# One hybrid decoder layer on one core: a new opening with diagonal transposes, larger pipelined side steps, and the second half of the cache staged through scratch

## The chip, the core and the metric

The kernel runs on one core of one Trainium2 chip, as one launch. The time is device microseconds of one execution, and the number compared is the median of several executions. Engines are named as in the profile: PE (TensorE matmul), PEld (its weight loads), DVE (VectorE), ACT (ScalarE), POOL (GpSimd), SP (SyncE, which here issues nearly all DMAs).

## The reference, cut to what matters

One layer of a hybrid decoder runs on 512 prompt tokens and on 32 sample tokens (8 sequences of 4), 544 columns in all. Every branch hangs on one input projection of the normalised tokens:

```
h = rmsnorm(x, norm_w)                    # 544 x 2048
zin = h @ w_in                            # 2048 x 14376, columns split into q, kv, gates, pool, conv, merge
# branch A: attention over compressed blocks, selected blocks and a window; the prompt reads its own keys,
#           a sample sequence reads 2048 past rows from 16 cache pages:
#           cache_kv[page] = 128 rows x (k_cmp, v_cmp, k_slc, v_slc) x 2 heads x 128
# branch B: causal pooling; branch C: conv and a chunked state-space scan
y = x + sum_b(sigmoid(G_b) * (m_b @ w_branch[b])) @ w_out
```

## The kernel before, in words

**Main units.** The projection is cut into tiles of 128 output columns, and each tile into four units of 4 x 128 contraction rows (a tile of the branch projection has two). A unit is one object with three calls: `dma()` loads 512 KB of weights (every second unit), `prep()` splits the weights into a high part `wh` (ACT) and a low part `wl` (DVE), and `mm()` issues 24 matmuls of 272 columns into the accumulator `zin` (wh x hhi, wl x hhi, wh x hlo, for two halves of the 544 columns). `hhi` and `hlo` are the normalised, transposed tokens in two parts. There are 612 units, and `run_units` walks through them: it loads six units ahead, prepares three units ahead, and then issues unit i.

**Side steps.** Everything else (norms of q and k, attention, pooling, convolution, scan, sample attention) is written as generators that stop at `yield`. After each unit, `run_units` adds `s.rate` to a counter and for each whole one takes one step of every generator in `s.sides`. The Tile scheduler then makes one instruction order for each engine out of this, and may pull instructions past each other where it thinks that one isn't ready. On PE the side matmuls therefore stand as insertions in a long row of `zin` matmuls. All side accumulators share four PSUM buffers (`s.A`, tag "a"), and most side data shares 32 SBUF buffers (`s.U`).

**Opening.** `x_prep` loads the sample tokens and four blocks of 128 prompt tokens, squares them (ACT), computes the reciprocal root (DVE, with one ACT Sqrt), scales the block by it and by `norm_w` (DVE, `scalar_tensor_tensor`), transposes it (PE, L156) into a tile `xT`, and splits it into `hhi` and `hlo`. The first unit needs all four blocks, since a matmul of 272 columns reaches across blocks. The first side generator, `tables`, loads constants and casts them on DVE (`trib`, `identb` and so on).

**Cache pages.** A page's number stands in a table, so a page load takes its address from a register that SP reads first (`value_load`). `stage_pages`, a side generator, copies columns 0 to 511 (the compressed keys and values) of 128 pages into scratch in HBM, `ckd`. The compressed kinds 0 and 1 are then loaded from `ckd` with fixed addresses, and the selected kinds 2 and 3 straight from the pages:

```
u = s.U("kr")
if kind < 2:                       # 256 KB from scratch, fixed address
    nc.sync.dma_start(u[:, :512]..., src[:, 4 * lq + e:4 * lq + e + 2, 256 * kind:256 * kind + 256])
if kind > 1:                       # 128 KB from the page whose number a register holds
    nc.sync.dma_start(u[:, o:o + 256], s.page(t, 4 * bl + e)[:, 256 * kind:256 * kind + 256])
```

SP issues DMAs strictly in its order: a weight load `wr` stands behind the `kr` loads issued ahead of it. The sample attention runs after the prompt attention `attn_p`: `samp_cmp` (keys `kT`, scores `cS`, values `pv`, `xvT`, `ocT`) twice, then `samp_group` four times (window and selected keys `kT`, scores `sS`, transposed probabilities `sP`, sums `sO`).

Of the kernel before, what the change touches and what calls it, by code (L numbers as in the profile page):

```python
# [29 lines left out]
RATE_SSD = 1.7  # L30
RATE_MG = 1.5
# [92 lines left out]
class Prog:  # L124
    def __init__(s, ctx, tc, a):
        s.ctx, s.tc, s.nc = ctx, tc, tc.nc
        s.a = a
        s.n = 0
        s.sides = []
# [67 lines left out]
    def setup(s):  # L197
# [8 lines left out]
        s.rate = 1.0  # L206
# [7 lines left out]
        s.ckd = [dt(f"ckd{b}", [16, 128, 512]) for b in range(8)]  # L214
# [15 lines left out]
    def params(s):  # L230
# [15 lines left out]
        s.nw = s.prm[:, 0:16]  # L246
# [10 lines left out]
        nc.vector.tensor_copy(s.trib, trineg)  # L257
        s.snegb = s.cp0.tile([32, 32], BF, name="snegb")
        nc.vector.tensor_copy(s.snegb, sneg[:32])
        s.identb = s.cp0.tile([128, 128], BF, name="identb")  # L260
        nc.vector.tensor_copy(s.identb, s.c("ident"))
        s.identr = s.cp0.tile([128, 128], R, name="identr")
        nc.vector.tensor_copy(s.identr, s.c("ident"))
# [3 lines left out]
    def x_prep(s):  # L267
        nc, a = s.nc, s.a
        X, J, W = {}, {}, []
        nw = a["norm_w"]  # L270
        row = lambda q, n: bass.AP(tensor=nw.tensor, offset=nw.offset + 512 * q, ap=[[0, n], [1, 512]])
        xs = s.U("xs")
# [3 lines left out]
        nc.sync.dma_start(s.cst[:, :128], a["cst_a"][:, :128])  # L276
        for i in range(4):
            X[i] = [s.U("x") for _ in range(4)]
            for q in range(4):
                nc.sync.dma_start(X[i][q][:, :512], a["x_prompt"][0, i * 128:i * 128 + 128, q * 512:q * 512 + 512])  # L280
            if i == 0:
                w4 = s.U("nw4")
                for q in range(4):
                    nc.sync.dma_start(w4[32 * q:32 * q + 32, :512], row(q, 32))
                mod, = s.cu("mod32")
                for q in range(4):
                    W.append(s.U("nw"))
                    nc.sync.dma_start(W[q][:, :512], row(q, 128))
        yield
# [3 lines left out]
        def square(x, o):  # L293
            j = s.U("junk")
            s.act(j[:, :512], x[:, :512], AF.Square, accum_out=o)


        ss = s.small(8)
        square(xs, ss[:, 0:1])
        p = s.A("xss")  # L300
        s.mm(p[:, :1], mod, ss[:, 0:1])
        nc.vector.tensor_copy(ss[:, 1:2], p[:, :1])
        s.rsqrt(ss[:, 2:3], ss[:, 1:2], 1.0 / DM, ss[:, 3:4])
        s.stt(xs[:, :512], xs[:, :512], ss[:, 2:3], w4[:, :512])
        p = s.A("xT")
        pv = p.rearrange("p (q e c) -> p e q c", q=4, e=4)
        for e in range(4):
            s.tr(pv[:, e], xs[:, e * 128:e * 128 + 128])
        s.hsplit(p.rearrange("p (k c) -> p k c", k=16), s.hhi[:, :, NP:T], s.hlo[:, :, NP:T])

        def norms(i):
            ss = J[i] = s.small(8)
            for q in range(4):
                square(X[i][q], ss[:, q:q + 1])

        def scale(i):
            ss = J.pop(i)
            nc.vector.tensor_reduce(ss[:, 4:5], ss[:, :4], axis=AX.X, op=OP.add)
            s.rsqrt(ss[:, 5:6], ss[:, 4:5], 1.0 / DM, ss[:, 6:7])
            for q in range(4):  # L320
                s.stt(X[i][q][:, :512], X[i][q][:, :512], ss[:, 5:6], W[q][:, :512])

        def turn(i):
            xs = X.pop(i)
            c = slice(i * 128, i * 128 + 128)
            for q in range(4):
                p = s.A("xT")
                for e in range(4):
                    s.tr(p[:, e * 128:e * 128 + 128], xs[q][:, e * 128:e * 128 + 128])
# [3 lines left out]
        for i in range(5):  # L333
            if i < 4:
                norms(i)
            if i:
                turn(i - 1)
# [1584 lines left out]
```

## Time and profile before

| | us |
|---|---|
| median of 3 runs (2452.2 to 2456.29) | 2454.61 |
| the profiled execution's own time | 2455.51 |
| its span, first to last instruction | 2453.7 |
| PE busy | 2381.8 (97%) |
| DVE busy | 1084.9 (44%) |
| ACT busy | 716.9 (29%) |
| POOL busy | 55.7 (2%) |

The profiled execution took 0.9 us more than the median, and 1.8 us of its time lie outside the span. PE is busy nearly all the time. Whatever shortens the kernel therefore takes away PE's idle time, makes its row of matmuls shorter, or lets it run at its faster clock for longer. In the tables of windows, PEclk is the granted clock as a share of 2.4 GHz: 0.50 is 1.2 GHz.

### The profile page before, as it was taken

To read this page: it belongs to the slowest core of one execution; us is meant where nothing else is said; L and a number is where in the kernel's file an instruction comes from. 1 tells how busy PE (TensorE), PEld (TensorE's weight loads), DVE (VectorE), ACT (ScalarE), POOL (GpSimd) and SP (SyncE) were. 2 spreads that over 40 slices of the span, in tenths; PEclk is the share of its full clock that TensorE was granted. 3 is DMA by queue.
4 is the path that set the end of the run, shared out by engine and by line. 5 is a ranking of instruction groups with operands and counts; after the bars stand their busy time and mean duration, and the time that the engine had idled before them with its cause. 6 is when DMAs were issued, how large, how long until landed. Compare 5 with 4: busy or idle time off the path is not lost. (4 is left out here: it accounts for less than half of the span.)

```text
span 2453.7 us, 49120 instructions
## 1 busy us (share of the span) xinstructions
PE 2381.8 (97%) x19749; PEld 2239.6 (91%) x19749; DVE 1084.9 (44%) x2206; ACT 716.9 (29%) x1369; POOL 55.7 (2%) x153
## 2 busy tenths in 40 slices
PE   4999999999999999999899999999999999999999
PEld 4999888888998998988798999989999999999999
DVE  5227547555332232423353545555446344445222
ACT  4222333333332222322232233322223322223221
POOL 0001011000000000000000000000000000000000
PEclk9999899999999999999999999999999999999999
DMA  7855563422568567665656543333646664443442
GB/s 213 243 160 147 168 173 99 136 69 75 154 202 246 159 192 227 174 196 162 208 160 196 143 126 89 102 105 111 183 128 196 183 189 132 133 133 99 127 132 81
DMA packets 525668, 377.27 MB, mean 154 GB/s; under 512 B 26895, under 2 KB 472615, under 8 KB 525440
## 3 DMA queue, kind: packets, MB, share of 16 engines
q1 hardware_dynamic: 518528, 360.76, 51.5%
q10 hardware_dynamic: 6912, 13.37, 1.5%
q8 instruction: 155, 2.54, 0.4%
q14 instruction: 73, 0.60, 0.1%
HBM read 328.31 MB, written 79.66 MB: 166 GB/s over the span
## 5 line engine op out<-in xcount | busy, mean ns | idle before, releaser
L153 PE MATMUL zin<-hhi,wh 128*128 128x272 f32 (+1 forms) x3616 | 784.6, 297 | 5.6 <-ACT wh L173 4.6
L176 DVE TENSOR_TENSOR wl<-wr,wh 128x512 fp32r<-128x512 f32 (+1 forms) x612 | 422.9, 693 | 776.4 <-ACT wh L173 772.9
L153 PE MATMUL zin<-hlo,wh 128*128 128x272 f32 (+1 forms) x3616 | 757.7, 290 | 0.0
L153 PE MATMUL zin<-hhi,wl 128*128 128x272 f32 (+1 forms) x3616 | 756.5, 290 | 0.2 <-DVE wl L176 0.2
L173 ACT ACTIVATE wh<-wr 128x512 fp32r<-128x512 f32 (+1 forms) x612 | 382.9, 628 | 1108.7 <-PE zin L153 919.5
L153 PEld LDWEIGHTS zin<-hhi,wh 128*128 128x128 f32 (+1 forms) x3616 | 568.3, 189 | 38.6 <-issue 28.3
L153 PEld LDWEIGHTS zin<-hhi,wl 128*128 128x128 f32 (+1 forms) x3616 | 570.2, 189 | 4.5 <-issue 3.0
L153 PEld LDWEIGHTS zin<-hlo,wh 128*128 128x128 f32 (+1 forms) x3616 | 567.8, 189 | 6.1 <-issue 5.2
L153 PE MATMUL zin<-bh,wh 128*128 128x272 f32 x1280 | 266.4, 290 | 1.1 <-DVE gt L185 1.1
L153 PE MATMUL zin<-bl,wh 128*128 128x272 f32 x1280 | 264.7, 288 | 0.0
L153 PE MATMUL zin<-bh,wl 128*128 128x272 f32 x1280 | 264.4, 288 | 0.0
L153 PEld LDWEIGHTS zin<-bh,wh 128*128 128x128 f32 x1280 | 200.0, 188 | 1.4 <-ACT wh L173 1.3
L153 PEld LDWEIGHTS zin<-bl,wh 128*128 128x128 f32 x1280 | 201.3, 189 | 0.0
L153 PEld LDWEIGHTS zin<-bh,wl 128*128 128x128 f32 x1280 | 201.1, 188 | 0.0
L1364 DVE COPY kT<-kT 128x512 f32<-128x512 f32 x72 | 49.0, 688 | 63.7 <-PE kT L156 63.1
L156 PE MATMUL kT<-cst,kr 128*128 128x128 f32 x512 | 68.9, 276 | 0.0
L156 PEld LDWEIGHTS kT<-cst,kr 128*128 128x128 f32 x512 | 56.6, 141 | 7.7 <-issue 5.7
L173 ACT ACTIVATE mg<-zin 128x544 f32<-128x544 f32 x48 | 29.8, 620 | 101.9 <-PE zin L153 101.9
L173 ACT ACTIVATE P<-S,sm 128x512 f32<-128x512 f32 (+3 forms) x64 | 33.8, 528 | 86.6 <-DVE sm L182 84.3
L173 ACT ACTIVATE kT<-kT 128x512 f32<-128x512 f32 x72 | 42.5, 595 | 33.8 <-PE kT L156 33.2
L153 PE MATMUL S<-kv,q 128*128 128x128 f32 (+3 forms) x128 | 47.1, 452 | 0.2
L153 PE MATMUL O<-PT,Vn 128*128 128x128 f32 x320 | 44.4, 277 | 0.0
(409 smaller groups left out, 1839.4 us busy)
## 6 DMA issues: line engine op xcount, KB each, us to landing
wr<-in_w_in_dram SPq DMA_DIRECT2D x224, 512.0 KB
ckd<-in_cache_kv_dram SPq DMA_DIRECT2D x128, 256.0 KB
kr<-ckd SPq DMA_DIRECT2D x128, 256.0 KB
kr<-in_cache_kv_dram SPq DMA_DIRECT2D x256, 128.0 KB
wr<-in_w_branch_dram SPq DMA_DIRECT2D x48, 512.0 KB
wr<-in_w_out_dram SPq DMA_DIRECT2D x32, 512.0 KB
mgd<-mg ACTq DMA_DIRECT2D x48, 272.0 KB
gt<-mgd SPq DMA_DIRECT2D x48, 272.0 KB
```

Source lines behind the costliest of these rows:

```text
L153: return s.nc.tensor.matmul(out, l, r, start=start, stop=stop, **kw)
L156: return s.nc.tensor.transpose(out, in_, s.c("ident")[:k, :k])
L173: return s.nc.scalar.activation(out, in_, f, **kw)
L176: return (eng or s.nc.vector).tensor_tensor(out, a, b, op=op)
L1364: s.nc.vector.tensor_copy(u[:, :NP], p)
```

## The change

Three things are done at once.

1. The opening is written anew and in an order fixed by hand (`manual_schedule` for ACT, DVE, PE and SP). Blocks 0 and 1 are loaded first. A block is no longer scaled on DVE. Its reciprocal root is multiplied into an identity matrix (`dg`), and an ordinary matmul of the block with that diagonal transposes and scales it in one; `norm_w` comes in when the result is split. The first tile's accumulator is split into 256 columns (blocks 0 and 1) and 288 columns (blocks 2, 3 and the samples), so that units 0 to 3 issue their first half (`part(q, 0)`) before blocks 2 and 3 are turned, and the second half (`part(q, 1)`) between their banks. Four casts of `tables` move from DVE to POOL.
2. Side steps are made larger: several old steps are one, and a step uses what the step before it produced. The rate falls from 1.0 (1.5 and 1.7 in places) to 0.55 (0.75 late). Page staging and the early loads of the branch stage move to a list of their own, `s.feeds`, which takes one step after each unit.
3. `stage_pages` copies both halves of the 128 pages into scratch (256 copies in place of 128), and the selected kinds are loaded from there, 128 loads of 256 KB in place of 256 of 128 KB.

```diff
-RATE_SSD = 1.7
-RATE_MG = 1.5
+RATE = 0.55
+RATE_SSD = 0.75
...
-        nc.vector.tensor_copy(s.trib, trineg)
+        nc.gpsimd.tensor_copy(s.trib, trineg)
...
+        load(0)
+        load(1)
+        units[0].dma()
+        units[2].dma()
...
+        def root(ss, n, i0):
+            v, r, t = ss[:, 16:16 + n], ss[:, 19:19 + n], ss[:, :n]
+            s.act(r, v, AF.Sqrt)
+            nc.vector.reciprocal(r, r)
...
+                s.ts(D[i0 + i][:, :128], ident, r[:, i:i + 1])
+        def split(*kpc):
+            for k, p, c in kpc:
+                s.act(s.hhi[:, k, c], p, scale=nwT[:, k:k + 1])
+            for k, p, c in kpc:
+                s.stt(s.hlo[:, k, c], p, nwT[:, k:k + 1], s.hhi[:, k, c].bitcast(F), OP.mult, OP.subtract)
...
+        def bankA(kb):
+            p = s.A("xT")
+            for h in range(2):
+                k = 2 * kb + h
+                for i in range(2):
+                    s.mm(p[:, h * 256 + i * 128:h * 256 + i * 128 + 128],
+                         X[i][k // 4][:, k % 4 * 128:k % 4 * 128 + 128], D[i][:, :128])
+            return p
...
+        bank = [bankA(kb) for kb in range(4)]
+        for kb in range(8):
+            split(*((2 * kb + h, bank[kb][:, h * 256:h * 256 + 256], slice(0, 256)) for h in range(2)))
+            if kb < 4:
+                bank.append(bankA(kb + 4))
+            if kb % 2:
+                units[kb // 2].prep()
+                part(kb // 2, 0)
+            if kb == 3:
+                square(xs, sc[:, 12:13])
+                p = s.A("xss")
+                s.mm(p[:, :1], mod, sc[:, 12:13])
+            if kb == 4:
+                nc.vector.memset(sc[:, 8:12], 0.0)
+                nc.vector.tensor_copy(sc[:, 8:9], p[:, :1])
+            if kb > 3:
+                i, q = divmod(2 * kb - 8, 4)
+                square(X[2 + i][q], sc[:, 4 * i + q:4 * i + q + 1])
+                square(X[2 + i][q + 1], sc[:, 4 * i + q + 1:4 * i + q + 2], True)
...
+        mean(sc, 3)
+        root(sc, 3, 2)
+        bank = [bankB(k) for k in range(4)]
+        for k in range(16):
+            split((k, bank[k][:, :288], slice(256, T)))
+            if k < 12:
+                bank.append(bankB(k + 4))
+            if k % 4 == 3:
+                part(k // 4, 1)
...
-                s.nc.sync.dma_start(s.ckd[b][i], s.page(t, i)[:, :512])
-                yield
+        for k in range(2):
+            for b in range(8):
+                t, nx = nx, s.ids((b + 1) % 8, 1, 0, 16)
+                for i in range(16):
+                    s.nc.sync.dma_start(s.ckd[k][b][i], s.page(t, i)[:, 512 * k:512 * k + 512])
+                    yield
...
                 units[i].mm()
+                s.feeds = [g for g in s.feeds if next(g, s) is not s]
                 acc += s.rate
...
+        for n in range(0, 36, 2):
+            for f, d in ((sc, 4), (sb, 2), (sa, 0)):
+                for m in (n - d, n - d + 1):
+                    if 0 <= m < 32:
+                        f(m)
             yield
...
+        for n in range(9):
+            if n:
+                scores(n - 1, kT)
+                kT = None
+            if n < 8:
+                kT = s.keys4(need(), CI)
+            yield
...
-            if j + 2 < 8:
-                W[j + 2] = s.cmp_w(1, j + 2)
+            if j + 3 < 8:
+                W[j + 3] = s.cmp_w(1, j + 3)
...
-            yield from keyT(need(), got)
+            p = scores(kT)
             u = s.U("sS")
...
+            if lq < 3:
+                kT = s.keys4(need(), CI)
+                yield
```

What the change does to the order, at three places. First DVE in the opening, before the change: the row in which the last block's root (the small `sm_298` rows) is mixed with weight splits `wl` and with the casts `trib` and `snegb` of the side generator.

```order
59 L176 TENSOR_TENSOR wl_354<-wr_151,wh_353 128x512
60 L191 RECIPROCAL sm_298<-sm_298 128x1
61 L176 TENSOR_TENSOR wl_358<-wr_153,wh_357 128x512
62 L176 TENSOR_TENSOR sm_298<-sm_298 128x1
63 L176 TENSOR_TENSOR wl_392<-wr_153,wh_391 128x512
64 L176 TENSOR_TENSOR sm_298<-sm_298 128x1
65 L257 CAST trib<-cu_430 128x128
66 L182 TENSOR_SCALAR sm_298<-sm_298 128x1
67 L259 CAST snegb<-cu_430 32x32
68 L176 TENSOR_TENSOR sm_298<-sm_298 128x1
```

The same engine in the opening after the change, between the fourth and the sixth bank of the first half (`hlo` rows are the low part of a turned bank, `junk` rows are squares, `xss` is PE's sum for the samples):

```order
23 L176 TENSOR_TENSOR wl_278<-wr_127,wh_277 128x512
24 L185 SCALAR_TENSOR_TENSOR hlo<-xT_229,sm_163,hhi 128x256 x2
25 L393 MEMSET sm_168 128x4
26 L394 COPY sm_168<-xss_295 128x1
27 L312 SCALAR_TENSOR_TENSOR junk_305,sm_168<-x_139 128x512
28 L185 SCALAR_TENSOR_TENSOR hlo<-xT_238,sm_163,hhi 128x256 x2
29 L176 TENSOR_TENSOR wl_312<-wr_129,wh_311 128x512
30 L312 SCALAR_TENSOR_TENSOR junk_329,sm_168<-x_141 128x512
```

The casts are gone from DVE, and the copy of `xss` now stands ahead of the rest of the first half's work.

Second, PE in the first group of the sample attention before the change: scores `sS` alone between two rows of main matmuls.

```order
4030 L153 MATMUL zin_12327<-hlo,wh_12230 128x272 x2
4031 L153 MATMUL sS_12409<-kT_12358,qs 32x512
4032 L153 MATMUL sS_12409<-kT_12365,qs 32x512
4033 L153 MATMUL sS_12409<-kT_12372,qs 32x512
4034 L153 MATMUL sS_12409<-kT_12379,qs 32x512
4035 L153 MATMUL zin_12327<-hhi,wh_12282 128x272 x2
```

PE at the like place after the change: behind the scores (their last row is the first here) stand, in one insertion, the transposes of the new keys and probabilities and those of the next 16 key tiles, in seven accumulators of the four buffers.

```order
4810 L153 MATMUL sS_15328<-kT_15252,qs 32x512
4811 L156 MATMUL nT_15336<-cst,nk_15095 16x128
4812 L156 MATMUL sP_15340<-cst,sW_15214 128x128 x4
4813 L156 MATMUL kT_15355<-cst,kr_14284 128x128 x2
4814 L156 MATMUL kT_15355<-cst,kr_14286 128x128 x2
4815 L156 MATMUL kT_15362<-cst,kr_14284 128x128 x2
4816 L156 MATMUL kT_15362<-cst,kr_14286 128x128 x2
4817 L156 MATMUL kT_15369<-cst,kr_14288 128x128 x2
4818 L156 MATMUL kT_15369<-cst,kr_14290 128x128 x2
4819 L156 MATMUL kT_15376<-cst,kr_14288 128x128 x2
4820 L156 MATMUL kT_15376<-cst,kr_14290 128x128 x2
4821 L153 MATMUL zin_15179<-hhi,wh_15175 128x272 x2
```

Counted over the whole order, PE goes over from main matmuls to an insertion 424 times before and 284 times after the change; from unit 4 on 420 and 278 times. The number of side matmuls from unit 4 on is the same but for two.

Third, SP where the selected rows of the first group are loaded, before the change: each load is preceded by the read of a page number.

```order
888 L350 TENSOR_LOAD pt_11640
889 L350 ISA x2
890 L375 ISA
891 L375 DMA kr_11707<-in_cache_kv_dram 128x256
892 L350 TENSOR_LOAD pt_11640
893 L350 ISA x2
894 L375 ISA
895 L375 DMA kr_11728<-in_cache_kv_dram 128x256
```

After the change such loads come from scratch, four for what were eight, next to the weights and small stores.

```order
1602 L447 DMA kr_17478<-ckd_91 128x2x256
1603 L447 DMA kr_17480<-ckd_91 128x2x256
1604 L447 DMA kr_17482<-ckd_92 128x2x256
1605 L447 DMA kr_17484<-ckd_92 128x2x256
1606 L489 DMA wr_17894<-in_w_in_dram 128x8x128
```

The reads of page numbers have moved to the staging, one page after each unit from unit 4 to unit 260. Measured in units, the prompt attention stands at units 86 to 136 before and 86 to 164 after, the two `samp_cmp` at 139 to 209 and 168 to 258, the four `samp_group` at 211 to 315 and 263 to 333. From unit 455 on (branch and output projection) the two orders do the same.

## Rows read from the trace of the kernel before

**Rows 1.** The page, part 1: engines, busy us, share, instructions.
```profile
PE 2381.8 (97%) x19749; PEld 2239.6 (91%) x19749; DVE 1084.9 (44%) x2206; ACT 716.9 (29%) x1369; POOL 55.7 (2%) x153
```

**Rows 2.** Waits of PE, whole run: us in total, times, longest.
```profile
PE xT L156 <- DVE x L185: 18.3, 5, 9.4
...
PE sS L153 <- ACT kT L173: 5.8, 2, 5.1
PE zin L153 <- ACT wh L173: 4.6, 1, 4.6
PE ocT L153 <- DMA cw<-in_cmp_w_dram: 4.2, 2, 3.4
PE pm L153 <- ACT pwh L173: 3.8, 1, 3.8
PE spT L156 <- ACT pu L173: 3.7, 1, 3.7
...
PE sO L153 <- ACT nT L173: 2.5, 1, 2.5
PE sS L153 <- DVE kT L1364: 2.0, 1, 2.0
```

**Rows 3.** Timeline of PE in the opening; at 60.11 unit 4 begins.
```profile
43.77 3.65 PE L156 MATMUL xT<-cst,x 128*128 128x128 f32 x16 [9.43 <-DVE x L185]
...
60.11 0.41 PE L153 MATMUL zin<-hhi,wh 128*128 128x272 f32 x2
```

**Rows 4.** Timeline of DVE in the opening.
```profile
11.04 0.16 DVE L302 COPY sm<-xss 128x1 f32<-128x1 f32 x1 [6.11 <-PE xss L153]
...
12.43 0.16 DVE L176 TENSOR_TENSOR sm<-sm 128x1 f32<-128x1 f32 x1
...
42.35 0.23 DVE L257 CAST trib<-cu 128x128 bf16<-128x128 f32 x1 [3.66 <-DMA cu<-in_cst_u_dram]
...
45.52 0.69 DVE L176 TENSOR_TENSOR hlo<-xT,hhi 128x512 fp32r<-128x512 f32 x1
```

**Rows 5.** Windows of the opening: engines' busy us, then PEclk, DMA share, GB/s.
```profile
0.00:10.00 10.00, 0.00 (x0) 0.00 (x0) 0.42 (x3) 2.93 (x6) 0.98 (x6) 1.00 0.65 190
...
40.00:48.00 8.00, 4.24 (x20) 4.26 (x21) 5.21 (x11) 2.35 (x4) 0.00 (x0) 0.50 0.55 154
```

**Rows 6.** Timeline of PE around one insertion, and around one of plain fp32 matmuls.
```profile
676.87 0.42 PE L153 MATMUL zin<-hlo,wh 128*128 128x272 f32 x2
677.12 1.04 PE L156 MATMUL kT<-cst,kr 128*128 128x128 f32 x8
677.91 0.49 PE L153 MATMUL zin<-hhi,wh 128*128 128x272 f32 x2
678.25 0.41 PE L153 MATMUL zin<-hhi,wl 128*128 128x272 f32 x2
...
794.84 1.95 PE L153 MATMUL ocT<-xvT,cw 128*128 128x128 f32 x16
```

**Rows 7.** The chain that ended last: a stretch without insertions.
```profile
1969.98 292.13 PE zin L153 x2328
```

**Rows 8.** Windows, columns as in rows 5.
```profile
300.00:600.00 300.00, 297.78 (x2446) 260.73 (x2445) 178.63 (x469) 104.43 (x244) 15.22 (x24) 1.00 0.40 114
755.00:790.00 35.00, 35.00 (x329) 30.35 (x322) 9.98 (x15) 10.10 (x17) 0.00 (x0) 1.00 1.06 311
1100.00:1200.00 100.00, 86.13 (x755) 78.20 (x754) 32.17 (x66) 24.81 (x55) 1.69 (x6) 0.97 0.59 172
1300.00:1400.00 100.00, 95.44 (x818) 88.66 (x819) 44.73 (x94) 27.89 (x56) 9.19 (x28) 0.98 0.60 173
```

**Rows 9.** Timeline of SP: page loads during the sample groups.
```profile
1108.61 8.67 SPq L375 DMA_DIRECT2D kr<-in_cache_kv_dram  x8
```

**Rows 10.** The tile kr, 600 to 1000 us: issue from scratch, ns min/median/max.
```profile
L371 SPq DMA_DIRECT2D kr<-ckd x128: 354/420/1457, 636.1 to 932.8; - x128
```

**Rows 11.** Timeline of ACT behind such page loads.
```profile
1194.63 1.15 ACT L173 ACTIVATE wh<-wr 128x512 fp32r<-128x512 f32 x2 [3.18 <-DMA wr<-in_w_in_dram]
```

More of the change, by code (lines that the diff above doesn't have):

```diff
@@ L275, in x_prep @@
             nc.sync.dma_start(xs[32 * q:32 * q + 32, :512], src[:, q * 512:q * 512 + 512])
[L276 to L288, printed above, removed]
-        yield
+        mod, = s.cu("mod32")
+        load(2)
+        load(3)
+        units[4].dma()
+        units[6].dma()
         dummy = s.small(1)
@@ L307, in x_prep @@
[L307 to L321, printed above, removed]
@@ new lines, in _opening, with part @@
+        ps = s.Z("zin")
+        def part(q, hf):
+            o, n = ((0, 256), (256, 288))[hf]
+            wh, wl = units[q].w
+            for k in range(4):
+                kk = 4 * q + k
+                xh, xl = s.hmov(kk)
+                for m, (w_, x_) in enumerate(((wh, xh), (wl, xh), (wh, xl))):
+                    s.mm(ps[:, hf, :n], w_[:, k], x_[:, o:o + n], kk == 0 and m == 0, kk == 15 and m == 2)
+        def bankA(kb):
[6 more added lines that the diff above has]
+            return p
@@ new lines, in bankB @@
+        def bankB(k):
+            p = s.A("xT")
+            q, e = divmod(k, 4)
+            for i in (2, 3):
+                s.mm(p[:, i * 128 - 256:i * 128 - 128], X[i][q][:, e * 128:e * 128 + 128], D[i][:, :128])
+            r = slice(32 * q, 32 * q + 32)
+            s.mm(p[:, 256:288], xs[r, e * 128:e * 128 + 128], D[4][r, r])
+            return p
+        sa, sb, sc = s.small(24), s.small(24), s.small(24)
+        for q in range(4):
+            square(X[0][q], sa[:, q:q + 1])
+        mean(sa, 1)
@@ new lines, in _opening @@
+        square(X[1][0], sb[:, 0:1])
+        root(sa, 1, 0)
+        for q in range(1, 4):
+            square(X[1][q], sb[:, q:q + 1], q == 2)
+        mean(sb, 1)
+        root(sb, 1, 1)
+        bank = [bankA(kb) for kb in range(4)]
[17 more added lines that the diff above has]
+                square(X[2 + i][q + 1], sc[:, 4 * i + q + 1:4 * i + q + 2], True)
@@ L1272, in m_norm @@
         for g in range(2):
-            P = [s.A("ms") for _ in range(2)]
+            Z = []
             for e in range(4):
@@ new lines, in sums @@
+        def sums(po, pt, raw, o, last):
+            for e in range(4):
+                for ci, bl, g in CI:
+                    v, c = raw[bl, e]
+                    c += o + g * 128
+                    s.mm(po[32 * ci:32 * ci + 32, :128], pt[:, e * 128 + 32 * ci:e * 128 + 32 * ci + 32],
+                         v[:, c:c + 128], False, last and e == 3, skip_group_check=True)
+        kT = s.keys4(wn, CI)
+        yield
+        p = s.A("vn")
+        for br in range(2):
+            s.tr(p[:16, br * 128:br * 128 + 128], vx[:, br])
@@ L1693, in open_e @@
     def open_e(s):
-        while s.sides:
+        while s.sides or s.feeds:
+            s.feeds = [g for g in s.feeds if next(g, s) is not s]
             s.step()
```

590 lines of the change are left out of this document (304 added, 286 removed).

## The prediction

> **What bounds the kernel now.** I first read the shares of busy time: PE is busy 97% of the span, no other engine half of it [rows 1]. So I read PE alone, in three views. The chain that ended last holds a stretch without insertions, 2328 main matmuls in 292.13 us, or 125.5 ns each [rows 7]. At that pace 14688 main matmuls are 1843 us, and the rest is insertions, waits and slow clock. The waits of PE come next [rows 2]: 18.3 us for scaled blocks in the opening, and later a handful of single stalls of 2 to 5 us. The windows show where the clock is lost: 0.50 late in the opening [rows 5], 0.97 and 0.98 in the two stretches with the long stalls [rows 8].
>
> **Term 1, the opening.** Unit 4 begins at 60.11 us [rows 3]; after the change units 0 to 3 are done inside the new opening, so its length is compared with that. What goes is plain: DVE stood 3.66 us for a constant behind which the last block's root and scaling waited [rows 4], and PE then idled 9.43 us and ran 16 transposes in 3.65 us, 0.228 each, twice the 0.13 or less of the eight in 1.04 us later on [rows 3, 6], with the granted clock at 0.50 [rows 5]. What comes, step by step:
>
> - Blocks 0 and 1 are about 2.2 MB with the constants. The queue moved 1.9 MB in its first 10 us [rows 5], so they have landed at about 10.5. Then the last square (about 0.7, as a 512-column row [rows 4]), a sum, the root (11.04 to 12.59, 1.55 us, for the like chain [rows 4]) and the diagonal: PE starts at 13.2.
> - A diagonal transpose is a plain fp32 matmul. Eight of 128 columns, in 16 records, took 1.95 us [rows 6], so 0.22 each with the tail taken off. A bank of the first half is four, 0.88 us. The first four banks I count at half speed, as the 16 transposes went [rows 3]: 7 us, to 20.
> - From there DVE sets the pace. It starts at 15.2, when the first bank is out and its high part copied. Its work in the first half is 16 rows of 256 columns at 0.42 (by the 0.69 of 512 columns [rows 4]), four `wl` and four squares at 0.69 and some small rows, together 12.8 us. Its order also puts the copy of `xss` ahead of half of that, and PE makes `xss` only behind the second part: DVE is through with bank 4 at 21.8 and PE with `xss` at 25, so 3.3 us are lost. That ends at 31.3; sum, root and three diagonals take 2.5 more: 33.8.
> - The second half is PE's again: 16 banks at 0.64 (two diagonals and a 32-column one that I take as 0.2) and 48 matmuls of 288 columns at 0.133 (125.5 ns x 288/272) are 16.6 us, against 16 x 0.43 + 3 x 0.69 = 9 us of DVE. Unit 4 begins at 50.4.
>
> The term is -9.7 us. Bounds: with no loss on DVE and full clock from the start, 44, or -16; with the second half at half clock, 67, or +7.
>
> **Term 2, fewer insertions.** Two pairs of main matmuls start 0.251 apart in the free stretch [rows 7]. The pair behind an insertion started at 677.91 and the next at 678.25, so 0.34: 0.09 us lost, while the pair ahead of it took its normal 0.25 [rows 6]. Insertions of column-tiled matmuls (`sO`, `cS`) have a longer entry and tail than this one, up to the 0.25 of a whole pair by my estimate. With 142 fewer insertions and nearly the same side matmuls, I take 0.11 each: -15.6 us, bounds -6 (half of the 0.09, since merged pieces may keep part of it) and -25.
>
> **Term 3, the stalls that go.** Seven lines of waits [rows 2]: `sS` on `kT` (5.8 and 2.0) and `sO` on `nT` (2.5), where a step used what it had just made and the new one uses the step before; `zin` on `wh` (4.6), `spT` on `pu` (3.7) and `pm` on `pwh` (3.8), where ACT itself waited for a transfer, as the 3.18 us for `wr` at 1194.63 [rows 11]; and `ocT` on `cw` (4.2), now loaded one piece further ahead. The second kind I lay to SP: eight page loads held its queue for 8.67 us, 1.08 each [rows 9], against 0.42 for a load from scratch [rows 10], and weights stand behind them. 256 of the first become 128 of the second, 54 us in place of 277, while 128 more copies are issued earlier, one for each unit of about 4 us, from a stretch in which PE idles 0.7% [rows 8]. All seven are 26.6 us. The clock lost beside them is 3 + 2 us (0.03 and 0.02 of 100 us [rows 8]). Term: -31.6, bounds -20 and -40.
>
> **Term 4, new stalls.** The stage `pv` fills the DMA queue already: 311 GB/s at a share of 1.06 in 35 us, with PE not idle [rows 8]. After the change its four steps take 7.3 units and move 8 MB of rows, 1.9 of weights, 1.9 of staging and some `cw`: 12.3 MB, 39.5 us at that rate, where PE's own work is about 35 us. 2 MB are loaded ahead, so of 2 x 4.5 us I count 4. Larger steps need five to seven accumulators from four buffers in one insertion. Attention before the change, where the buffers are also full, idles 2.2 of 300 us [rows 8]; the same 0.7% over the 1000 us that larger steps cover is 7 us. Term: +11, bounds 0 and +40. POOL's four casts and the DVE time saved cost nothing, since neither engine bounds.
>
> **Sum.** The profiled time is 2453.7 + 1.8 = 2455.5 us. 2455.5 - 9.7 - 15.6 - 31.6 + 11 = 2409.6; the median of the runs lies 0.9 under the profiled one, so 2409 us.
>
> **Rivals.**
>
> *The stalls only move.* If the sample groups, now packed into 70 units in place of 104, stall on weights as before, term 3 falls to -10 and term 4 stays: 2430. For it: the two stretches with stalls lie where pooling and sample groups overlap, and they still do for most of it. Against it: SP's time falls to a fifth there.
>
> *The opening stays at half clock.* In the new opening PE works in bursts with pauses of about 2 us. In the old one the clock was 0.50 after a pause of 9.43 us [rows 3, 5], and no row shows what short pauses do in a stretch half empty. At half clock to the end the second half takes 33 us: unit 4 begins at 67, the other terms stay, 2426. The Trainium skill bears on this: its page "TensorE: Matmul & The Clock Gate", section "HAM oscillation — how this bites in real kernels", says that short bursts between waits put PE back to half rate again and again. By that rule this rival would be the forecast; the trace agrees for the long pause alone, and the stall of 3.7 and the one of 4.6 us near 1190 cost the 100 us around them only 0.03 of the clock [rows 2, 8], so I keep it a rival.
>
> *Nothing new stalls.* Term 4 near zero and the opening at its better bound: 2409 - 11 - 6 = 2392.
>
> *The four buffers decide (slower than before).* An insertion that needs more than four accumulators waits for a copy out, 0.69 us on DVE [rows 4], and DVE runs in order behind two weight splits. About 120 steps of attention and sample attention are of this kind. The gain without term 4 is 57 us, so 0.48 us in each of the 120, less than one copy late, turns the change into a loss; at one copy each, 83 us, it is 2481. For it: seven accumulators stand in one insertion of the new order. Against it: PE's attention idles 0.7% with the buffers full [rows 8], and copies alternate between DVE and ACT, both under half busy [rows 1].
>
> **Chances and range.** The forecast, 2397 to 2420, has 0.52; stalls that only move 0.15; half clock 0.13; nothing new 0.12; the buffers 0.08, of which part stops short of a loss. The range 2390 to 2438 leaves out the buffers, and the ends of the others. A difference of under 0.2% (5 us) can't be told from none by this measurement. Faster 0.91, same 0.03, slower 0.06, from the same cases.
>
> **What would show it.** Opening: the first matmul of 272 columns near 50 us, a DVE wait for `xss` of about 3 us, and PEclk of 1.00 from 20 us on. Insertions: from unit 4 to the end PE's row shorter by 15 us once waits are taken off. Stalls: no `zin` on `wh`, `pm` on `pwh` or `spT` on `pu` over 1 us between 1100 and 1400. New ones: waits of `pv` or `ocT` on `kr` or `cw` near units 200 and 250, and waits of PE on `kT`, `PT` or `sP` copies of less than 0.7 us each. I am wrong if `kr` or `wr` makes PE wait through the whole staging, units 132 to 260, or if the clock drops in the packed sample groups.

## The result, and the profile after

The changed kernel takes 2401.56 us (median of 6 runs, 2396.29 to 2406.27), the kernel before 2456.22 beside it: ratio 0.9776, 95% interval 0.9765 to 0.9787. The forecast was 2409. The profiled execution took 2404.53 us, so it is 51.0 us under that of before. That total is close to the forecast, in part by luck: one term missed by 14 us one way, two others together by 17 us the other way.

Engines of the changed kernel, from the page (answers to [rows 1]):

```profile
PE 2370.6 (99%) x19842; PEld 2247.1 (94%) x19842; DVE 1088.2 (45%) x2204; ACT 723.1 (30%) x1374; POOL 64.5 (3%) x157
```

PE's waits in the changed kernel (answers to [rows 2]):

```profile
PE xT L153 <- DVE dg L181: 12.3, 3, 8.2
PE zin L153 <- DVE wl L176: 4.3, 3, 2.0
...
PE gn L156 <- DVE kv L185: 2.0, 1, 2.0
...
PE pv L153 <- DMA kr<-ckd: 1.3, 3, 0.7
```

None of the seven lines that term 3 named is left. The new ones are small: `pv` on `kr` never waits over 0.7 us, the only accumulator that PE waits for in the sample groups is `spT`, 0.4 us, and the longest wait behind the opening is `gn` on `kv`, 2.0. Of the 32.2 us in which PE idles now, 19.1 lie in the opening, 8.7 between unit 4 and PE's end, and the rest behind PE's end.

The opening of the changed kernel, PE (answers to [rows 3]); unit 4 begins at 64.75:

```profile
28.83 0.39 PE L153 MATMUL zin<-hhi,wl 128*128 128x256 f32 x1 [2.02 <-DVE wl L176]
...
32.22 0.39 PE L153 MATMUL zin<-hhi,wl 128*128 128x256 f32 x1 [1.71 <-DVE wl L176]
...
35.28 1.22 PE L153 MATMUL xT<-dg,x 128*128 128x128 f32 x4 [1.49 <-DVE dg L181]
...
36.99 1.22 PE L153 MATMUL xT<-dg,x 128*128 128x128 f32 x4
...
64.75 0.41 PE L153 MATMUL zin<-hhi,wh 128*128 128x272 f32 x2
```

And DVE's wait ahead of the first pause (answer to [rows 4]):

```profile
26.62 0.16 DVE L394 COPY sm<-xss 128x1 f32<-128x1 f32 x1 [2.73 <-PE xss L153]
```

PE paused for 2.02, 1.71 and 1.49 us. In the second half a bank then starts 1.71 us after the one before (35.28 to 36.99). The windows of the changed kernel say why (columns as in [rows 5]; the first is the opening's slow part, the second the sum over the two stretches at half clock from unit 4 to PE's end, at 226.4 and 284.4, the third all from unit 4 to PE's end, and the last two answer to [rows 8]):

```profile
35.20:52.30 17.10, 17.02 (x62) 14.72 (x63) 4.56 (x11) 4.00 (x8) 0.00 (x0) 0.50 0.29 83
...
sum 6.80, PE 6.80 PEld 6.78 DVE 3.78 ACT 0.90 POOL 1.35; mean PE 3.40 PEld 3.39 DVE 1.89 ACT 0.45 POOL 0.68
...
64.75:2398.42 2333.67, 2324.96 (x19585) 2205.98 (x19583) 1059.96 (x2124) 695.47 (x1306) 63.01 (x149) 1.00 0.59 171
...
1100.00:1200.00 100.00, 100.00 (x876) 93.49 (x875) 54.43 (x112) 33.28 (x69) 4.10 (x14) 1.00 0.54 163
...
1300.00:1400.00 100.00, 99.49 (x920) 91.55 (x919) 55.78 (x128) 35.45 (x75) 7.87 (x23) 1.00 0.75 229
```

The same windows of the kernel before: from unit 4 to PE's end, one stretch at half clock away from any stall, and the sum over all five stretches at half clock there (at 256.5, 1096.1, 1191.7, 1341.9 and 1809.5).

```profile
60.11:2449.58 2389.47, 2353.05 (x19583) 2213.49 (x19581) 1051.57 (x2118) 690.39 (x1304) 54.69 (x147) 0.99 0.53 152
...
256.50:270.20 13.70, 13.70 (x89) 10.89 (x89) 3.77 (x16) 3.45 (x10) 0.00 (x0) 0.50 0.13 46
...
sum 30.70, PE 27.08 PEld 20.73 DVE 10.53 ACT 7.85 POOL 0.00; mean PE 5.42 PEld 4.15 DVE 2.11 ACT 1.57 POOL 0.00
```

So the 51.0 us come apart like this. The opening costs 64.75 - 60.11 = 4.6 us more. From unit 4 to PE's end 2389.47 became 2333.67, 55.8 less. Of these, 27.7 are PE's idle time (36.42 to 8.71). PE's busy time fell by 28.1, of which 13.5 - 3.4 = 10.1 are the slow clock (half of the 27.08 and of the 6.80 us that PE was busy at 0.50), and 18.0 are left for the shorter row of matmuls.

Two of these parts can be held against the other runs below. Taken in the same way, the row of matmuls from unit 4 on is 2339.5 us in the kernel before and 2340.7 in `new_opening_only`, and 2319.3 to 2322.6 in the changed kernel and the seven others that have both the larger steps and the scratch and nothing added to the branch stage, so some 18 us are found again. The 10.1 us of clock are less sure. Of the 13.5 us lost before, 5.0 lie at the stalls of [rows 2] (near 1096, 1192 and 1342 us), and the others away from them. Those differ between executions: the 13.7 us at half clock at 256.5 were 3.4 in `new_opening_only`, which does the same work there, and the 6.8 us of the changed kernel were 17.1 in `copy_late`.

### The profile page after: what moved, and what is told of

It is laid out like the page before. It is cut to its first block, busy times and chain, and to the rows that moved or that the text cites. A ratio compares the mean times of both kernels' runs of the same rounds, so it can differ in the third digit from the quotient of the medians.

```text
span 2402.8 us, 48653 instructions
## 1 busy us (share of the span) xinstructions
PE 2370.6 (99%) x19842; PEld 2247.1 (94%) x19842; DVE 1088.2 (45%) x2204; ACT 723.1 (30%) x1374; POOL 64.5 (3%) x157
## 4 chain that ended last, share of the span: by engine, by line
PE 94%; DVE 2%; DMA 2%; issue 1%; ACT 0%; POOL 0%; SPq 0%; DVEq 0%; ACTq 0%
PE zin L153 74%; PE kT L156 3%; PE O L153 2%; PE S L153 2%; PE xT L153 1%; PE y L153 1%; PE sO L153 1%; PE sS L153 1%; PE PT L156 1%; PE cS L153 1%; PE ns L153 1%; PE ocT L153 1%; DMA kr<-ckd 1%; PE qw L153 1%; DVE rp L176 1%
## 5 line engine op out<-in xcount | busy, mean ns | idle before, releaser
L153 PE MATMUL zin<-hhi,wh 128*128 128x272 f32 (+2 forms) x3616 | 774.5, 294 | 0.0
L153 PE MATMUL zin<-hhi,wl 128*128 128x272 f32 (+2 forms) x3616 | 756.2, 289 | 4.3 <-DVE wl L176 4.3
L153 PE MATMUL zin<-hlo,wh 128*128 128x272 f32 (+2 forms) x3616 | 756.4, 290 | 0.0
L156 PEld LDWEIGHTS kT<-cst,kr 128*128 128x128 f32 x512 | 55.7, 141 | 11.7 <-issue 10.1
L173 ACT ACTIVATE kT<-kT 128x512 f32<-128x512 f32 x72 | 42.7, 596 | 55.8 <-PE kT L156 55.1
L185 DVE SCALAR_TENSOR_TENSOR gt<-gt,zin 128x544 f32<-128x544 f32 x32 | 23.1, 721 | 48.1 <-PE zin L153 46.4
L173 ACT ACTIVATE P<-S,sm 128x128 f32<-128x128 f32 (+3 forms) x64 | 33.8, 528 | 36.8 <-DVE sm L182 22.8
```

The source lines that it names most:

```text
L153: return s.nc.tensor.matmul(out, l, r, start=start, stop=stop, **kw)
L156: return s.nc.tensor.transpose(out, in_, s.c("ident")[:k, :k])
L173: return s.nc.scalar.activation(out, in_, f, **kw)
L185: return s.nc.vector.scalar_tensor_tensor(out, a, sc, b, op0=op0, op1=op1)
```

## The experiments

All times are medians of 5 runs (11 for `new_opening_only`) with the ratio to the kernel before on the same chip, unless a single run is said; `unit 4 at` is read from the one profiled execution of each kernel. The changed kernel at its 0.9776 is 2400.2 beside a kernel before of 2455.2.

### The opening: what let the clock fall

**copy_late**: DVE's copy leaves its place in the fifth bank.

```diff
-            if kb == 4:
-                nc.vector.memset(sc[:, 8:12], 0.0)
-                nc.vector.tensor_copy(sc[:, 8:9], p[:, :1])
...
+        nc.vector.memset(sc[:, 8:12], 0.0)
+        nc.vector.tensor_copy(sc[:, 8:9], p[:, :1])
         mean(sc, 3)
```

> The changed kernel with DVE's copy of the samples' sum moved from the fifth bank of the first half to the end of that half. Theory (DVE's wait of 2.73 us for that sum delays the rest of the half): the wait goes, the three diagonals are done near 32.9 in place of 35.6, PE's pause of 2.02 us goes, and the clock still falls to half at the start of the second half, since pauses remain: unit 4 near 62.0, total 2399. Rival 1 (the pause of 2.02 us was the one that let the clock fall): clock 1.00 through the second half, unit 4 near 55, total 2392. Rival 2 (DVE's wait is covered by something else, such as the loads of blocks 2 and 3): diagonals at 35.6 as before, 2401.6.

**fill_pauses**: extra matmuls on PE ahead of the three pauses (17, 14 and 12).

```diff
+        fz = s.Z("fill")
+        def idle(q, n):
+            for _ in range(n):
+                s.mm(fz[:, 0, :256], units[q].w[0][:, 0], s.hmov(0)[0][:, :256])
...
+                idle(kb // 2 - 1, (0, 0, 17, 14)[kb // 2])
                 part(kb // 2, 0)
...
+        idle(3, 12)
         bank = [bankB(k) for k in range(4)]
```

> The changed kernel with 43 extra 256-column matmuls on PE in the opening, 17, 14 and 12 of them ahead of the three pauses of 2.02, 1.71 and 1.49 us; they write an accumulator that nobody reads. Theory (the clock fell because of the pauses): it stays at 1.00, a bank of the second half starts 0.98 us after the one before in place of 1.71, unit 4 begins near 57.4, and the total is 7.3 us shorter, 2394. Rival (the clock falls with the kind of work that the second half begins with, whatever stands ahead of it): 0.50 from 35.2 us on for some 17 us as before, unit 4 near 65, total 2402.

**copy_late_fill**: both edits, with 4, 14 and 12 extra matmuls.

> Both edits: the copy at the end of the first half, and 4, 14 and 12 extra matmuls ahead of the three places where PE paused. Theory (a wait of 2.7 us on DVE and a clock loss of 7.3 us, which add up): clock 1.00 throughout, unit 4 near 54.8, total about 10 us shorter than the changed kernel, 2391.5. Rival (the two overlap, since the wait on DVE made the pauses and so the clock loss): no better than the better of the two edits alone.

| | time, us | ratio | 95% interval | unit 4 at, us |
|---|---|---|---|---|
| changed kernel | 2401.56 | 0.9776 | 0.9765 to 0.9787 | 64.75 |
| copy_late | 2400.53 | 0.9780 | 0.9766 to 0.9793 | 62.23 |
| fill_pauses | 2397.05 | 0.9762 | 0.9749 to 0.9775 | 57.22 |
| copy_late_fill | 2392.96 | 0.9753 | 0.9740 to 0.9766 | 54.81 |

PE in `fill_pauses`, the first two banks of the second half and unit 4:

```profile
35.13 0.71 PE L153 MATMUL xT<-dg,x 128*128 128x128 f32 x4
36.11 0.71 PE L153 MATMUL xT<-dg,x 128*128 128x128 f32 x4
...
57.22 0.41 PE L153 MATMUL zin<-hhi,wh 128*128 128x272 f32 x2
```

The banks start 0.98 us apart, and the clock stays at 1.00 through the opening: PE did more work and was done 7.5 us earlier. So the pauses let the clock fall, and not the kind of matmul behind them. The other profiled executions agree. In seven kernels the opening's pauses aren't filled (the changed kernel, `copy_late` and five below), and the clock fell to 0.50 in each of them, for 6.8 to 23.9 us in all, with unit 4 at 57.85 to 66.05. In the three with filled pauses it held 1.00.

`copy_late` took DVE's wait away as expected, with unit 4 2.5 us earlier, but two pauses were left (0.86 and 1.41 us) and 17.1 us at half clock with them. In its median these 2.5 us don't show: 0.9780 against 0.9776. Together the two add up in the profiled executions, with unit 4 at the 54.8 us that were expected.

By the ratios of the medians the gains are smaller than expected: 3.4 us for `fill_pauses` (7.3 expected, and the intervals overlap) and 5.6 us for both edits (10 expected). What filling is worth depends on how much clock the opening loses in an execution. The mean granted clock of a whole run was 0.992 to 0.997 in the six runs of the changed kernel, and 0.996 to 0.998 in the five of `fill_pauses`.

**samples_one_bank**: on top of both edits, the second half built like the first. Two k of blocks 2 and 3 share a bank, and the samples are turned by four full diagonals in one bank. One square moves from DVE to ACT.

```diff
-            for i in (2, 3):
-                s.mm(p[:, i * 128 - 256:i * 128 - 128], X[i][q][:, e * 128:e * 128 + 128], D[i][:, :128])
-            s.mm(p[:, 256:288], xs[r, e * 128:e * 128 + 128], D[4][r, r])
...
+        for e in range(4):
+            s.mm(pS.rearrange("p (q e c) -> p e q c", q=4, e=4)[:, e], xs[:, e * 128:e * 128 + 128], D[4][:, :128])
...
+        s.tt(v, pS.rearrange("p (k c) -> p k c", k=16), nwT[:, :, None].to_broadcast([128, 16, 32]))
+        s.hsplit(v, s.hhi[:, :, NP:T], s.hlo[:, :, NP:T])
```

> The copy late and the extra matmuls of before, and the second half of the opening like the first: two k of blocks 2 and 3 in one bank, the sample tokens turned by four diagonal matmuls in one bank of their own in place of sixteen pieces of 32 x 32, and one square moved from DVE to ACT. Theory (the second half is bound by PE's row, and its banks cost 0.98 us because of the small sample pieces in each): eight banks of 0.98, 1.0 for the samples and 48 x 0.133 for the main matmuls are 15.2 us in place of 22.1, unit 4 near 47.5 in place of 54.8, total 2385.5. Rival (a bank of two k takes twice a bank of one, so only the sixteen sample pieces of 0.33 less 1.0 go): unit 4 near 50.5, 2388.5.

It took 2386.45 us, ratio 0.9721 (0.9707 to 0.9734), the fastest kernel here. PE in its second half:

```profile
32.50 1.95 PE L153 MATMUL xT<-dg,x 128*128 128x128 f32 x16
34.29 1.06 PE L153 MATMUL xT<-dg,xs 128*128 128x128 f32 x8
35.18 2.84 PE L153 MATMUL xT<-dg,x 128*128 128x128 f32 x24
...
47.16 0.41 PE L153 MATMUL zin<-hhi,wh 128*128 128x272 f32 x2
```

Eight diagonals (16 records) now take 34.29 - 32.50 = 1.79 us, 0.224 each, which is the 0.22 that the forecast took. Unit 4 begins at 47.16 (expected 47.5). A bank with a 32 x 32 piece cost 0.98, so the piece alone cost about 0.53, by the difference to two full diagonals.

### The opening in other company

**new_opening_only**: the kernel before with `x_prep` and `fill` replaced by `opening` and the four casts moved to POOL, and nothing else.

> The kernel before with the new opening and POOL's four casts, and nothing else of the change. Theory (by itself the new opening costs time, since half clock takes what DVE's wait gave): unit 4 near 64.8 us in place of 60.11, total 4.6 us longer than before, ratio 1.002. Rival (the new opening gains in any company, as the 12.6 us suggest by which the old opening under the new steps was slower than the changed kernel): about 2442, ratio 0.995.

2457.91 us, ratio 1.0009 (0.9999 to 1.0018), unit 4 at 64.19. Alone the new opening gains nothing: it is 4.1 us longer by unit 4, 2.7 us in the median, and the interval includes 1. It also has 17.1 us at half clock, from 34.6 on.

**old_opening**: the changed kernel with `opening` replaced by `x_prep` and `fill`.

> The larger steps and the staging through scratch, with the opening of the kernel before. Theory (the new opening cost time, and all of the gain lies behind it): unit 4 begins near 60.1 us in place of 64.75, and the whole is about 4.6 us shorter than the changed kernel, 2397 us (ratio to before 0.976). Rival 1 (where unit 4 begins does not carry through to the end): same as the changed kernel, 2401.6. Rival 2 (the new opening gains as forecast, by what it leaves loaded for the units behind it): about 2411.

2414.2 us, ratio 0.9844 (0.9829 to 0.9858): 14 us slower than the changed kernel. Unit 4 begins at 64.94 and not near 60.1, so the theory fails at its first step; the time is nearest to that of rival 2. DVE in it (beside the 3.66 us of [rows 4]), and SP ahead of it:

```profile
47.23 0.23 DVE L256 CAST trib<-cu 128x128 bf16<-128x128 f32 x1 [7.50 <-DMA cu<-in_cst_u_dram]
```

```profile
41.70 1.85 SPq L361 DMA_DIRECT2D ckd<-in_cache_kv_dram  x2
...
45.35 0.36 SPq L169 DMA_DIRECT2D cu<-in_cst_u_dram  x1
```

The staging, now in `s.feeds`, starts with unit 0 of the old opening, and its page copies stand on SP ahead of the constant `cu` that holds DVE up.

**old_opening_feed_late**: the same, with `s.feeds.append(s.late(8, s.stage_pages()))`, which lets eight units pass first.

> The larger steps with the old opening as in the run old_opening, but the staging of pages begins eight units later, so that its loads stand behind the constants on SP. Theory (there the old opening was slow because SP issued page loads ahead of the constant that DVE waits for, 7.50 us in place of 3.66): the wait falls to 4 us or less, unit 4 near 61, total near 2409. Rival 1 (the constant is late because its side steps come at the rate of 0.55): the wait stays at 7 to 8, total 2414. Rival 2 (what remained above the changed kernel was the opening alone): 2400.

2408.85 us, ratio 0.9814 (0.9800 to 0.9827): the wait for `cu` is back at 3.44 us and unit 4 at 59.45, so the staging ahead of the constant was the cause of the late unit 4. This kernel reaches unit 4 5.3 us before the changed one and is still some 9 us slower. From there to PE's end (59.45 to 2402.98, busy 2330.95) PE idles 12.6 us in place of 8.7 and is busy 6.0 us longer, with 17 us at half clock between 228 and 325 in place of 6.8. The clock need not come from the opening: `copy_late` and `fill_pauses` have 17 us at half clock there too, and are 8 to 12 us faster. The idle time lies above the 6.4 to 9.5 us of the six kernels that have the larger steps, the scratch and the new opening, and nothing added to the branch stage. Why it does isn't settled.

### The staging through scratch

**pages_direct**: the changed kernel with `rows`' selected kinds taken from the pages again.

```diff
-                    s.nc.sync.dma_start(s.ckd[k][b][i], s.page(t, i)[:, 512 * k:512 * k + 512])
+                s.nc.sync.dma_start(s.ckd[b][i], s.page(t, i)[:, :512])
...
+            if kind > 1:
+                nc.sync.dma_start(u[:, o:o + 256], s.page(t, 4 * bl + e)[:, 256 * kind:256 * kind + 256])
```

> The changed kernel with the selected rows loaded straight from the pages again (256 loads of 128 KB with an address from a register, 128 staging copies fewer). Theory (the page loads hold SP and with it the weights): waits of zin on wh, pm on pwh and spT on pu come back while the selected rows are loaded, 8 to 15 us with their clock, 2410 to 2417. Rival (the larger steps alone had removed these waits): within 2 us of the changed kernel, 2399 to 2404.

2491.93 us, ratio 1.0143 (1.0129 to 1.0157): 92 us slower than the changed kernel and slower than the kernel before, far beyond the 8 to 15 expected. SP, and then ACT, in the sample groups:

```profile
1369.39 8.84 SPq L448 DMA_DIRECT2D kr<-in_cache_kv_dram  x8
...
1382.43 8.65 SPq L448 DMA_DIRECT2D kr<-in_cache_kv_dram  x8
1391.13 6.02 SPq L490 DMA_DIRECT2D wr<-in_w_in_dram  x3
```

```profile
1395.11 1.15 ACT L173 ACTIVATE wh<-wr 128x512 fp32r<-128x512 f32 x2 [11.53 <-DMA wr<-in_w_in_dram]
```

ACT stood 11.53 us for a weight that SP issued at 1391.13, behind sixteen page loads. From unit 4 to PE's end this kernel takes 2423.80 us with PE busy for 2355.77: 59 us more of idle time and 31 more of busy time than the changed kernel; 23 of the 31 are slow clock (PE was busy at 0.50 for 52.6 us in place of 6.8), and the other 8 are not explained.

The likely reason for the size is the packing: 32 x 8.67 = 277 us of SP's time [rows 9] would have to fit into 70 units of about 4 us, where there were 104 before. The trace fits this: the page loads run from 1072.4 to 1548.5 us, 476 us, about as long as the 493 us before (941.1 to 1434.1), though the units are fewer. No run packs them less, so this is argued and not shown.

The traces also show what holds SP in these 1.08 us for each load. The DMA instruction itself takes 0.33 us (median of 256 in the kernel before), less than the 0.42 of a load from scratch, which brings twice the bytes. The rest goes into the page's number and the address made from it, 0.27 us into reading the number alone (median of 192). So what left the sample groups with the staging is mainly the reading of numbers. Reading them earlier while loading straight from the pages was not tried.

**scratch_only**: the kernel before with both halves of the pages staged and read from `ckd`; one page per step for the first half, two for the second.

> The kernel before, small steps and old opening, with both halves of the pages staged and the selected rows loaded from scratch. Theory (page loads hold SP): the waits of zin on wh (4.6), pm on pwh (3.8) and spT on pu (3.7) go, and with them about 3 us of clock; those of the small steps stay: about 15 us shorter than before, 2440, ratio 0.994. Rival (these waits come from where the small steps stand, not from SP): ratio 0.999 to 1.001.

2448.11 us, ratio 0.9965 (0.9951 to 0.9978): half of the 15 expected. In the profiled execution PE idles 12.5 us less from unit 4 on (36.4 to 23.9) but is busy 8.2 us longer, of which 1.7 are slow clock; what the other 6.5 are isn't known. PE's waits from 700 to 1400 us in it:

```profile
PE zin L153 <- ACT mg L173: 5.8, 2, 3.3
PE wT L156 <- DMA cw<-in_cmp_w_dram: 4.3, 2, 4.0
PE ocT L153 <- DMA cw<-in_cmp_w_dram: 3.9, 2, 2.2
PE zin L153 <- ACT wh L173: 1.3, 1, 1.3
```

The waits of `spT`, `pm` and (but for 1.3 us) of `zin` on `wh` went. So did those of `sS` on `kT` and `sO` on `nT`, though the small steps stayed. New ones stand at 805 to 860 us (the two of `ocT` among them, which stood near 965 before), where the staging now issues page copies in fours, 4.36 us each time, between the `cw` and `wr` loads. ACT and SP in the kernel before, at the `sS` stall of 5.1 us at 1096.07, show why these went too:

```profile
1094.90 0.63 ACT L173 ACTIVATE wh<-wr 128x512 fp32r<-128x512 f32 x1 [5.96 <-DMA wr<-in_w_in_dram]
1095.44 0.58 ACT L173 ACTIVATE kT<-kT 128x512 f32<-128x512 f32 x1
```

```profile
1081.48 8.67 SPq L375 DMA_DIRECT2D kr<-in_cache_kv_dram  x8
1090.20 0.43 SPq L423 DMA_DIRECT2D wr<-in_w_in_dram  x1
```

The copy `kT` stood on ACT behind a weight split that waited for a weight, which stood on SP behind eight page loads. The view of waits names ACT's copy; the chain behind it begins at SP. The waits of `sS` at 1134.67 and of `sO` at 1155.56 have the same chain: ACT had waited 12.82 and 2.43 us for a weight there, and SP had issued that weight behind page loads.

### The four buffers, and the price of an insertion

**copies_twice**: each of the 144 copies of `kT` out of PSUM is made twice (`for _ in range(2):` around it).

> The changed kernel with each of the 144 copies of turned keys out of PSUM made twice, so that each of the four buffers that holds one is held 0.6 to 0.7 us longer; the second copy writes the same values. Theory (the four buffers have more than one copy of slack, which is why the larger steps brought no waits): PE waits less than 5 us more, total under 2406. Rival (the buffers only just suffice): in each of the 36 insertions with four such copies PE waits for about two of them, 36 x 1.3 = 47 us, 2448.

2404.67 us, ratio 0.9794 (0.9780 to 0.9807): 4.4 us more than the changed kernel. In its profiled execution PE idles 6.9 us from unit 4 on (57.85 to 2396.27, busy 2331.49), no more than the 8.7 of the changed kernel. Its busy time is 6.5 us longer, which is about what its slow clock costs (20.5 us at 0.50 in place of 6.8), so the 4.4 us are no waits for buffers. So the buffers that hold turned keys have more than a copy of slack.

**insertion_price** and **insertion_kinds** (a single run each): extra matmuls in the branch stage, where 24 main matmuls take 24 x 125.5 ns = 3.012 us [rows 7].

```diff
+        p = s.A("pr")
+        for j in range(k):
+            o = p[:, j * 128:j * 128 + 128]
+            if b < 2:
+                s.tr(o, wt[:, j].bitcast(F))
+            else:
+                for ci in range(4):
+                    s.mm(o[32 * ci:32 * ci + 32], s.cst[:, 32 * ci:32 * ci + 32], wt[:, j].bitcast(F), skip_group_check=True)
```

> The changed kernel with extra matmuls in the branch stage, where a row of 24 main matmuls else takes 3.012 us: over 16 units one transpose behind each, over 16 units four transposes behind every fourth, over 16 units four column-tiled matmuls of 32 x 128 behind each, and over 16 units sixteen of them behind every fourth; nobody reads them. The same work in a quarter of the insertions, so each pair of stretches differs by 12 insertions. Theory (an insertion costs 0.11 us beside its work): 16 units with 16 insertions take 1.1 us more than with 4 for the transposes, 1.5 to 3 us more for the column-tiled ones. Rival (most of the 18 us of term 2 is in the side matmuls' own rows): under 0.4 us of difference.

> As in insertion_price, with other extra work, which nobody reads: over 16 units one plain fp32 matmul of 128 x 128 behind each, over 16 units four of them behind every fourth, over 16 units four transposes and four column-tiled matmuls in turn behind each unit (16 insertions), and over 16 units the same eight together behind every second (8 insertions). Theory (what an insertion costs hangs on its kind: nothing for transposes and 0.34 us for column-tiled ones, as insertion_price showed, and something between for plain fp32): 16 insertions of plain fp32 take 0.6 to 2.5 us more than 4; the mixed stretches differ by under 0.4 us, since the eight column-tiled entries stay. Rival (only column tiling costs): plain fp32 under 0.2 us of difference. Rival (each merge saves some 0.1): the mixed stretches differ by 0.8 us or more.

PE in `insertion_price`: single transposes; fours of them, four units apart; column-tiled fours (8 records), a unit apart; sixteens (32 records), four units apart. Where the second row of a pair counts fewer records than the first, the view ends inside that insertion.

```profile
1992.34 0.27 PE L156 MATMUL pr<-cst,wh 128*128 128x128 f32 x1
1995.47 0.27 PE L156 MATMUL pr<-cst,wh 128*128 128x128 f32 x1
...
2051.38 0.60 PE L156 MATMUL pr<-cst,wh 128*128 128x128 f32 x4
2063.86 0.60 PE L156 MATMUL pr<-cst,wh 128*128 128x128 f32 x4
...
2092.36 0.43 PE L153 MATMUL pr<-wh,cst 128*32 128x128 f32 x8
2095.93 0.32 PE L153 MATMUL pr<-wh,cst 128*32 128x128 f32 x4
...
2158.47 1.08 PE L153 MATMUL pr<-wh,cst 128*32 128x128 f32 x32
2171.73 0.53 PE L153 MATMUL pr<-wh,cst 128*32 128x128 f32 x12
```

One transpose adds 3.13 - 3.01 = 0.11 us, four together 12.48 - 12.05 = 0.43, so 0.11 each as well: the insertion itself costs next to nothing. Column-tiled, four add 3.57 - 3.01 = 0.56 and sixteen 13.26 - 12.05 = 1.21. Twelve more cost 0.65, or 0.054 each, and 0.34 of the first 0.56 is the insertion. So over 16 units, sixteen insertions of transposes take 0.1 us more than four (1.1 were expected, under 0.4 by the rival), and sixteen column-tiled ones 4.1 us more (1.5 to 3 were expected).

PE in `insertion_kinds`: plain fp32, one per unit and four per four units; then transposes and column-tiled fours in insertions of their own, and both in one.

```profile
1991.40 0.38 PE L153 MATMUL pr<-cst,wh 128*128 128x128 f32 x2
1994.64 0.38 PE L153 MATMUL pr<-cst,wh 128*128 128x128 f32 x2
...
2052.16 1.05 PE L153 MATMUL pr<-cst,wh 128*128 128x128 f32 x8
2065.07 0.61 PE L153 MATMUL pr<-cst,wh 128*128 128x128 f32 x4
...
2094.85 0.60 PE L156 MATMUL pr<-cst,wh 128*128 128x128 f32 x4
...
2101.87 0.60 PE L156 MATMUL pr<-cst,wh 128*128 128x128 f32 x4
...
2154.02 0.60 PE L156 MATMUL pr<-cst,wh 128*128 128x128 f32 x4
...
2161.04 0.60 PE L156 MATMUL pr<-cst,wh 128*128 128x128 f32 x4
```

Plain fp32 costs 3.24 - 3.01 = 0.23 alone and (12.91 - 12.05) / 4 = 0.215 in fours, so next to nothing for the insertion. Over 16 units, sixteen insertions of it take no longer than four (under 0.1 us), as the rival had it for column tiling alone, where 0.6 to 2.5 us were expected. Two units with transposes and column-tiled matmuls take 7.02 us either way, as expected. Merging saves only where it takes away a change to column tiles.

## Why the prediction was right, and where it was not

The total and its sign were right. By its own steps:

**Term 1, the opening (-9.7), was wrong: +4.6 in the profiled execution.** The step that failed is "full clock" in the second half, which was kept as a rival with 0.13 (unit 4 at 67). It came true in part: the clock was 0.50 for 17.1 of the second half's 29.5 us and not to its end, and unit 4 at 64.75 lies so near the rival's 67 only because the next step failed too. `fill_pauses` shows the cause, and for this execution the size: 7.5 us. The Trainium skill ("TensorE: Matmul & The Clock Gate", "HAM oscillation — how this bites in real kernels") tells of bursts shorter than the waits between them, with PE back at half rate after every wait. Here pauses of 2.02, 1.71 and 1.49 us, about as long as the bursts of 1.7 and 1.6 us between them, were enough, so the trace goes further than that case. The prediction left out that the section's waits are the longer part; the section by itself doesn't say that pauses like these matter. I let two later stalls in a busier stretch weigh too much. The second step is the cost of a bank, 0.64 taken and 0.98 measured, 5.4 us over 16 banks: the sample piece was put at 0.2 and cost 0.53. The third is a start 1.5 us late (35.28 for 33.8). Together 14.4, the whole miss of 14.3 in this execution; in that of `copies_twice` the same opening was done 6.9 us sooner. DVE's wait for `xss` was right (2.73 for 3.3).

**Term 2, fewer insertions (-15.6), was right in size, and its price was wrong.** 18.0 us are left for it, and other runs repeat that. But 0.11 us for each insertion is right at best as a mean of two kinds: nothing for transposes and plain matmuls, 0.34 for column-tiled ones. I read 0.09 us off the pair behind an insertion of transposes, and didn't set against it that this pair begins early, ahead of the end of the transposes' own row. Counted over the order, changes from 128-column tiles into tiles of 32 columns or fewer fell from 174 to 142: 32 x 0.34 = 10.9 us by estimate. What the other 7 us are was not tried.

**Term 3, the stalls that go (-31.6), was right for the stalls that it named.** All seven lines went, 26.6 us, and the clock beside them cost the 5.0 us that were taken. Idle time and clock together are -37.8, with the little of term 4 in it. The 6 us that the term didn't have are mostly clock lost away from these stalls, which differs between executions. Its first kind, a step that "used what it had just made", was a misreading: `scratch_only` removes the `sS` and `sO` waits with the small steps in place, since they too hung on a weight behind page loads.

**Term 4, new stalls (+11), did not come.** `pv` waits for `kr` 1.3 us in all (4 taken) and the buffers cost 0.4 in the sample groups (7 taken); `copies_twice` shows the slack. The 11 us that didn't come and the 6 us of clock paid for the miss of term 1; that they are of like size is luck.

**The rivals.** Stalls that only move: behind the opening no line of waits is over 2.0 us. The four buffers: excluded for the turned keys. Nothing new stalls: true, but for the opening's better bound. What the prediction didn't see is that the parts need each other. Scratch alone gives 0.9965, the larger steps without it 1.0143 (with the new opening in it), all three 0.9776.

## What to carry to other kernels

When an engine's copy makes PE wait, look at what that engine itself stood behind, down to the DMA queue; packing the steps closer without freeing the queue first made the kernel slower. In a stretch where PE waits for another engine again and again, price the work behind it at half clock too, and try matmuls that nobody reads in the pauses. Count what an insertion costs by the tile shape that it changes to, not by its number.

## What the runs showed of the hardware that was not expected

The granted clock behind the same opening differs between executions. In the changed kernel it was 0.50 for 17.1 us from 35.2 on; in `copies_twice`, whose opening has the same code, for 6.8 us from 29.5 on, and unit 4 began at 57.85 in place of 64.75:

```profile
29.50:36.30 6.80, 5.51 (x24) 4.89 (x23) 5.18 (x19) 0.21 (x1) 0.00 (x0) 0.50 0.18 52
```

```profile
57.85 0.41 PE L153 MATMUL zin<-hhi,wh 128*128 128x272 f32 x2
```

These 6.9 us are of the size of the spread of the changed kernel's runs (10 us). The longest such stretch, in `insertion_price`, was 23.9 us from 30.6 on. With the pauses filled, three executions of three kernels held 1.00 through the opening. A change from full-width tiles to 32-column ones and back costs 0.34 us of PE's row, and a 32 x 32 piece in a row of full diagonals 0.53 where the full diagonal costs 0.224.
